# Where the low parts of split weights are made: VectorE alone, or GpSimd in two stages

## The chip, the cores and the metric

The kernel runs on one core of a Trainium2 chip. The core has a matrix engine (PE in the profile), a vector engine (DVE), a scalar engine (ACT), GpSimd (POOL) and a sync engine (SP) that issues the DMAs. The metric is the device time of one execution in microseconds; below it stands as the median of three runs.

## The reference

Two transformer blocks follow each other, each with two layers, on 256 tokens of width 1024 (the first block also carries a second stream of 256 context tokens). Cut to what matters here:

```python
# first block, layer l
h  = modulate(rms_norm(x,  norm1_g[l]), sh1, sc1)      # and hc from the context stream
q, k, v, up, ca, cb = split(h @ w_in[l])               # the same for hc
attn   = diff_attention(rope(q), [kc, rope(k)], [vc, v])
pool_o = pool_mixer(up, ...)
conv_o = conformer_conv(ca, cb, ...)                   # 31 taps, depthwise
x = x + g1 * concat(attn, pool_o, conv_o) @ w_out[l]
x = x + g2 * swiglu(modulate(rms_norm(x, norm2_g[l])), w_ffn_in[l], w_ffn_out[l])
# second block, layer l
c_q, c_kv, k_r, q_d, k_d, v_d = split(rmsnorm(x) @ w_in_2[l])
o_a = mla_mixer(c_q, c_kv, k_r, ...)                   # 8 heads, dense attention
o_b = dilated_attention(q_d, k_d, v_d, rel_bias)       # 8 heads
x = x + concat(o_a, o_b) @ w_out_2[l]
x = x + conv_ffn(rmsnorm(x), w_up_2[l], ...)
```

All of it is in float32.

## The kernel before

A product with a weight is made in three passes on the matrix engine. Weights come in **pieces** of at most 128 x 1024 elements: SP loads a piece into a tile `raw` (four buffers), ACT rounds it into the high part, `hl[:, 0]` (L202), and VectorE subtracts that from `raw` to make the low part, `hl[:, 1]` (L204). `hl` has four buffers as well. The activations have a high and a low part too, and PE adds high x high, high x low and low x high into one PSUM bank (L156). A piece therefore costs ACT one cast, VectorE one subtraction with two inputs in SBUF, and PE its products; PE's first product of a piece needs the high part alone, its second the low part.

`dense` is the loop for a projection: for each piece, for each tile of 128 tokens, for each k-slice of the piece, the three products. In the first layer's q, k and v there are four token tiles and a piece holds two k-slices of 512 columns, so a piece feeds 24 products.

Program order is written with generators. `weave(main, side, rate)` advances the main generator and, for each of its steps, `rate` steps of a side generator. The framework then places the instructions in the engines' queues by their order in the program and by a simulated time at which each becomes ready: an instruction that is ready early can be put ahead of ones that stand before it in the code. Each engine works its queue in order.

Three places matter here.

*The first layer's q, k, v stage* (`layer1` with `l == 0`). Main makes q, k and v out of twelve pieces (two of them already split by `start`); the side runs ten steps of `conv_mix`, the depthwise convolution on VectorE: per channel half 31 taps, one `tensor_scalar` and thirty `scalar_tensor_tensor` (L1236), each 128 x 512 with two inputs in SBUF. Ten steps cover 43 of the 62 taps; the others stand in the side generator of the next weave. After the stage two pieces for the pooling branch are split (`pool_pieces`), then `diff_attention` starts: for each head, score products on PE, a maximum on VectorE (L1297, from PSUM), exponentials on ACT (L1299), a combination on VectorE (L1304), and two heads later transposes and value products on PE.

*The second block's attentions* (`layer2`, both layers). Before them stand the projections to q, k and v of the first attention; their last VectorE steps scale the keys (L1631, L1633) ahead of PE's transposes. Then main runs 8 + 8 heads and the side runs the projection of the second attention's keys (4 pieces), of its values (4 pieces) and the first four pieces of the output projection.

*GpSimd* makes only small reciprocal roots (L162, L163, L421, L422) and memsets in the kernel before.

Of the kernel before, what the change touches and what calls it, by code (L numbers as in the profile page):

```python
# [9 lines left out]
F32 = mybir.dt.float32  # L10
# [87 lines left out]
class _Kernel:  # L98
    def __init__(self, ctx, tc, io, out):
        self.tc, self.nc, self.io, self.out = tc, tc.nc, io, out  # L100
        self.n = 0
        self.last = self.mark = None
        self.later, self.due = [], []
        pool = lambda name, bufs, **kw: ctx.enter_context(tc.tile_pool(name=name, bufs=bufs, **kw))
        self.big = pool("big", 12)
        self.wraw = pool("wraw", 4)
        self.whl = pool("whl", 4)
        self.s4 = pool("s4", 3)
        self.s2 = pool("s2", 6)
        self.small = pool("small", 16)  # L110
        self.cst = pool("cst", 1)
        self.lay = pool("lay", 1)
        self.gatep = pool("gatep", 2)
        self.setp = pool("setp", 1)
        self.junkp = pool("junkp", 1)
        self.conv = pool("convp", 1)
        self.acc = pool("acc", 4, space=bass.MemoryType.PSUM)
        self.aux = pool("aux", 3, space=bass.MemoryType.PSUM)
        self.ob = pool("ob", 1, space=bass.MemoryType.PSUM)
        self.dram = pool("dram", 1, space=DRAM)  # L120
# [73 lines left out]
    def piece(self, view, a, b, mark=None):  # L194

        return self.split(self.load(view, a, b), a, b, mark)

    def split(self, raw, a, b, mark=None):
        nc = self.nc
        n = a * b  # L200
        hl = self.whl.tile([P, 2, 1024], F32R, tag="hl", name=self.nm("hl_"))
        nc.scalar.copy(hl[:, 0, :n], raw[:, :n])  # L202
        with self.behind(mark):
            nc.vector.tensor_sub(hl[:, 1, :n], raw[:, :n], hl[:, 0, :n].bitcast(F32))  # L204
        hi = hl[:, 0, :n].rearrange("p (a b) -> p a b", a=a)
        lo = hl[:, 1, :n].rearrange("p (a b) -> p a b", a=a)
        return hi, lo
# [744 lines left out]
    def layer1(self, l, S, xin, hT, first=()):  # L952

        nc, io = self.nc, self.io
# [16 lines left out]
        def band_load():  # L971
            band = self.A8([P, 2, 4, SEQ])
            for kt in range(2):
                self.dma(band[:, kt], io["k_band"][kt].rearrange("p (g t) -> p g t", g=4))
            return band
# [10 lines left out]
        def values(ready):  # L986
            v.append(self.A8([P, 4, 512]))
            yield from self.dense(
                stat, KD, w_in, 1024, 1536, kv_toks, lambda t, j, b: nc.scalar.copy(v[0][:, t, :], b), ready=ready)

        def main():
            kp, pp, vp = [], [], []
            ahead_v = lambda: vp.append(piece(0, 2, 1024, 1536))
            yield from self.qk_chunk(S, 0, stat, w_in, q_toks, qT, rq, "q_norm_g", first,
                                     lambda: kp.append(piece(0, 2, 512, 1024)))
            yield from self.qk_chunk(S, 1, stat, w_in, kv_toks, kT, rq, "k_norm_g", kp,
                                     (lambda: pp.extend(pool_pieces())) if last else ahead_v)
            if last:
                yield from self.pool_mix(S, stat, 0, band, mB, pp, ahead_v)
            yield from values(vp)  # L1000

        if last:
            band = band_load()
            self.weave(main(), conv, TAPS[l])
        else:

            self.weave(main(), (next(conv) for _ in range(10)), 0.84)
        self.flush()
        v = v[0]
# [4 lines left out]
        def add(gts):  # L1014
            last = [None]

            def evac(t, n, b):
                cs = slice(n * 512, (n + 1) * 512)
                tmp = self.S2([P, 512])
                with self.behind(last[0]):  # L1020
                    nc.vector.tensor_mul(tmp, b, gts[t // 2][:, cs])
                r = res[t // 2][:, t % 2, cs]
                last[0] = nc.vector.tensor_add(r, r, tmp)  # L1023
                return last[0]
            return evac

        hT2 = None
        if not last:
            gates = [self.gate(l, 2, s) for s in streams]

            band, pp = band_load(), pool_pieces()

            def side():
                for s in streams:
                    for _ in self.pool_mix(S, stat, s, band, mB, pp):
                        next(conv, None)
                        yield
                mA.extend(self.parts(TQ))
                for _ in conv:
                    yield  # L1040
                yield from self.ada_rows(l, 2)
                self.rows_to_gates(gates)
                for p, d in ((3, 2), (4, 3)):
                    yield from self.ada_rows(l, p)
                    self.rows_to_cols(S.mod[:, d], S.part(p))

            rf = lambda t: res[t // 2][:, t % 2, :]
            out = self.out_proj(mstat, io["w_out"][l], TQ, add(gates), lambda t: done(t))

            def side_all():  # L1050
                yield from side()
                while not self.fronts:
                    yield
                for _ in range(2):
                    next(out)
                    yield

            self.weave(self.diff_attention(S, qT, kT, v, rq, q_toks, mA, LAG), side_all(), 2.0)
            for s, name in enumerate(("x", "ctx")):
                res[s] = self.reload(name)  # L1060
            G2, S2 = self.modulation(S, l, 1, "n2")
            hT2 = self.norm_out(512)
            done = self.norm_step(rf, G2, S2, hT2)
            for _ in out:
                pass
            g2, nxt = [None, None], []

            def side2():
                yield
                yield  # L1070
                for s in streams:
                    g2[s] = self.gate(l, 5, s)
                nxt.append(self.setup1(l + 1))
                yield from self.ada_sums(l, 5, streams)
                self.sums_to_gates(g2)
                nx = nxt[0]
                nx.rest()
                yield from self.setup2()
                self.gate_next = self.gate(l + 1, 2, 2)
                for p, d, st in ((0, 0, [0, 1]), (1, 1, [0, 1]), (3, 2, [0]), (4, 3, [0])):  # L1080
                    yield from self.ada_sums(l + 1, p, st)
                    self.sums_to_cols(nx.mod[:, d], nx.part(p))
                yield from self.ada_sums(l + 1, 2, [0])
                self.sums_to_gates([self.gate_next])

            end = {}

            def done_ffn(t):
                if t == 0:
                    end["hT"] = self.norm_out(512)  # L1090
                    end["step"] = self.norm_step(rf, *self.modulation(nxt[0], l + 1, 0, "n1"), end["hT"])
                end["step"](t)

            self.weave(
                self.ffn_wide(hT2, io["w_ffn_in"][l], io["w_ffn_out"][l], self.glu(512), add(g2), done_ffn),
                side2(), 0.85)
            return nxt[0], res[0], end["hT"]
# [398 lines left out]
    def layer2(self, l, S, xres, bias, begin):  # L1496
        nc, io = self.nc, self.io
# [147 lines left out]
        def drain(g):  # L1645
            for _ in g:
                pass
# [75 lines left out]
        def main():  # L1723
            yield from attention(
                lambda h, t: qT[0:MQK, h, t * P:(t + 1) * P], lambda h: kT[0:MQK, h, :], mrq, None, 0)
            yield from attention(
                lambda h, t: dqT[sl(h), h // 2, t * P:(t + 1) * P], lambda h: dkT[sl(h), h // 2, :], drq,
                lambda h, t: bias[t][:, h, :], 1)
# [10 lines left out]
        def side():  # L1739
            yield from dil_chunk(1, base + 512, dkT)  # L1740
            self.flush()
            yield from self.dense(
                stat, KD, w_in, base + 1024, base + 1536, toks,
                lambda t, j, b: nc.scalar.activation(vv[:, 1, t, :], b, AF.Identity, scale=rs[t]))
            while len(turned) < 4:
                yield
            for _ in range(4):
                next(out)
                yield
                yield  # L1750

        self.weave(main(), side(), 1.2)
        drain(out)
        nxt, end = [], {}

# [54 lines left out]
```

## Time and profile before

| what | value |
|---|---|
| median of three runs | 1667.15 us (1663.48 to 1668.55) |
| the profiled execution's own time | 1667.61 us |
| its span, first to last instruction | 1665.8 us |
| PE busy | 1618.0 us (97%) |
| VectorE busy | 1180.4 us (71%) |
| ACT busy | 793.9 us (48%) |
| GpSimd busy | 43.8 us (3%) |
| TensorE's granted clock, mean | 0.983 of full speed |
| subtractions L204 on VectorE | 382, busy 457.8 us |

Busy is the share of the span in which an engine had an instruction under way; a busy PE may still be waiting inside a group of products. The time before and after the span (1667.61 less 1665.8) is 1.8 us.

### The profile page before, as it was taken

The numbers are of one execution on the slowest core, as the hardware profiler recorded it, in microseconds if no ns is written. First come the engines' busy times: TensorE is split into PE (matmuls) and PEld (weight loads), VectorE is DVE, ScalarE is ACT, GpSimd is POOL, SyncE is SP. The second block draws the span as 40 slices with busy tenths as digits, with TensorE's granted clock in tenths as the row PEclk, the third lists the DMA queues.
The fourth block names the chain that finished last, engine by engine and source line by source line (L and its number), as shares of the span: only waits on it lengthen the run. The fifth ranks groups of instructions, "written<-read, shape, count | busy, mean of one in ns | idle before, by whom it ended". The sixth has DMA issues, their size and how long they took to land.

```text
span 1665.8 us, 24269 instructions
## 1 busy us (share of the span) xinstructions
PE 1618.0 (97%) x9241; PEld 1354.8 (81%) x9241; DVE 1180.4 (71%) x2130; ACT 793.9 (48%) x1347; POOL 43.8 (3%) x99
## 2 busy tenths in 40 slices
PE   7999999999999999999799899999999999999999
PEld 5787568878888888886698899767999987689998
DVE  4796656856575555986566457877887888778786
ACT  4334436323222224655543346765555577665554
POOL 1000000000000000000000001000000010000000
PEclk8999979999999999999899999999999999999999
DMA  9421651745375553432369655432656554246553
GB/s 329 129 89 59 245 177 55 225 148 168 108 228 174 175 153 113 140 114 82 99 224 243 194 188 159 151 102 88 204 181 190 177 150 150 87 128 189 189 181 122
DMA packets 183011, 262.71 MB, mean 158 GB/s; under 512 B 11277, under 2 KB 122864, under 8 KB 182896
## 3 DMA queue, kind: packets, MB, share of 16 engines
q1 hardware_dynamic: 182616, 260.85, 50.1%
q8 instruction: 72, 1.18, 0.3%
q10 hardware_dynamic: 280, 0.33, 0.2%
q14 instruction: 43, 0.35, 0.1%
HBM read 259.84 MB, written 1.31 MB: 157 GB/s over the span
## 4 chain that ended last, share of the span: by engine, by line
PE 69%; DVE 12%; issue 8%; DMA 6%; ACT 3%; POOL 1%; SPq 0%; POOLq 0%; ACTq 0%; DVEq 0%
PE aux L156 34%; PE acc L156 27%; PE ob L156 6%; DVE hl L204 3%; DMA raw<-in_w_mod_dram 3%; PE aux L248 2%; DVE a L1236 2%; DVE s L1236 1%; ACT hl L202 1%; DMA a<-dbias 1%; DMA raw<-in_w_ffn_out_dram 1%; DVE s L355 1%; DMA raw<-in_w_in_dram 1%; ACT s L461 1%; DVE sm L843 1%
## 5 line engine op out<-in xcount | busy, mean ns | idle before, releaser
L156 PE MATMUL acc<-hl,a 128*128 128x512 f32 (+3 forms) x3072 | 720.4, 387 | 8.1 <-ACT hl L202 2.9
L156 PEld LDWEIGHTS acc<-hl,a 128*128 128x128 f32 x3072 | 553.5, 190 | 127.2 <-issue 15.5
L202 ACT CAST hl<-raw 128x1024 fp32r<-128x1024 f32 (+2 forms) x382 | 393.6, 1036 | 473.5 <-PE aux L156 141.4
L156 PE MATMUL aux<-a,hl 128*128 128x256 f32 (+1 forms) x4032 | 578.5, 304 | 8.1 <-ACT a L462 2.9
L156 PEld LDWEIGHTS aux<-a,hl 128*128 128x128 f32 x4032 | 539.4, 192 | 41.5 <-ACT a L462 3.7
L204 DVE TENSOR_TENSOR hl<-raw,hl 128x1024 fp32r<-128x1024 f32 (+2 forms) x382 | 457.8, 1203 | 162.0 <-ACT hl L202 160.3
L355 DVE SCALAR_TENSOR_TENSOR s<-raw,csf,s 128x1024 f32<-128x1024 f32 x70 | 88.7, 1281 | 46.8 <-DMA raw<-in_w_mod_dram 46.7
L248 PEld LDWEIGHTS aux<-km,s 128*128 128x128 f32 (+1 forms) x384 | 45.2, 143 | 35.9 <-issue 20.1
L248 PE MATMUL aux<-km,s 128*128 128x128 f32 (+1 forms) x384 | 60.0, 284 | 12.3 <-DVE s L443 8.0
L156 PE MATMUL ob<-a,hl 128*128 128x512 f32 (+1 forms) x288 | 64.3, 372 | 0.0
L156 PEld LDWEIGHTS ob<-a,hl 128*128 128x128 f32 x288 | 51.2, 188 | 9.4
L524 ACT ACTIVATE s<-aux 128x512 f32<-128x512 f32 x33 | 19.7, 598 | 66.0 <-PE aux L156 66.0
L552 ACT ACTIVATE s<-s,c2a,c2b 128x256 f32<-128x256 f32 x88 | 48.0, 593 | 5.9 <-DVE s L549 5.9
L527 ACT CAST a<-s 128x512 fp32r<-128x512 f32 x33 | 20.4, 618 | 54.9 <-DVE s L526 54.8
L549 DVE TENSOR_TENSOR s<-aux,km 128x512 f32<-128x512 f32 x44 | 30.4, 691 | 20.5 <-PE aux L156 20.5
L1236 DVE SCALAR_TENSOR_TENSOR a<-up,c,a 128x512 f32<-128x512 f32 x60 | 43.5, 748 | 0.5
L525 DVE SCALAR_TENSOR_TENSOR s<-s,aux 128x512 f32<-128x512 f32 x33 | 22.6, 685 | 29.4 <-ACT s L524 29.4
L248 PE MATMUL aux<-km,a 128*128 128x128 f32 (+1 forms) x196 | 31.1, 289 | 10.5 <-ACT a L770 7.9
L409 ACT ACTIVATE jk<-a 128x512 bf16<-128x512 f32 x44 | 28.1, 640 | 25.2 <-DVE a L1023 19.7
L553 DVE SCALAR_TENSOR_TENSOR s<-s,c2a,s 128x255 f32<-128x255 f32 x88 | 38.7, 479 | 1.4 <-ACT s L552 1.4
L248 PEld LDWEIGHTS aux<-km,a 128*128 128x128 f32 (+1 forms) x196 | 23.7, 146 | 18.6 <-ACT a L770 8.1
L555 DVE SCALAR_TENSOR_TENSOR s<-s,c2b,s 128x255 f32<-128x255 f32 x88 | 38.7, 480 | 0.1
(257 smaller groups left out, 1364.3 us busy)
## 6 DMA issues: line engine op xcount, KB each, us to landing
raw<-in_w_ffn_in_dram SPq DMA_DIRECT2D x88, 512.0 KB
raw<-in_w_up_dram SPq DMA_DIRECT2D x88, 512.0 KB
raw<-in_w_in_dram SPq DMA_DIRECT2D x60, 512.0 KB
raw<-in_w_mod_dram SPq DMA_DIRECT2D x56, 512.0 KB
raw<-in_w_ffn_out_dram SPq DMA_DIRECT2D x44, 512.0 KB
raw<-in_w_down_dram SPq DMA_DIRECT2D x44, 512.0 KB
wm<-in_w_mod_dram SPq DMA_DIRECT2D x16, 1024.0 KB
raw<-in_w_out_dram SPq DMA_DIRECT2D x32, 512.0 KB
```

The source lines that it names most:

```text
L156: self.nc.tensor.matmul(o, lhsT, rhs, start=start, stop=stop)
L202: nc.scalar.copy(hl[:, 0, :n], raw[:, :n])
L204: nc.vector.tensor_sub(hl[:, 1, :n], raw[:, :n], hl[:, 0, :n].bitcast(F32))
L248: self.nc.tensor.transpose(b[:rows, j * P:(j + 1) * P], s, self.ident)
L355: self.nc.vector.scalar_tensor_tensor(accs[s], raw, c, accs[s], op0=ALU.mult, op1=ALU.add)
L409: self.nc.scalar.activation(junk, x[:, h * 512:(h + 1) * 512], AF.Square, scale=D ** -0.5, accum_out=ss[:, h:h + 1])
L525: nc.vector.scalar_tensor_tensor(th, th, 1.0, g, op0=ALU.add, op1=ALU.mult)
L549: nc.vector.tensor_mul(y, x.rearrange("p (j t) -> p j t", j=2), R2)
L552: nc.scalar.activation(o[:, j, :], y[:, j, :], AF.Identity, scale=wc(1, ff), bias=bc(ff))
L553: nc.vector.scalar_tensor_tensor(o[:, j, 1:SEQ], y[:, j, 0:SEQ - 1], wc(0, ff), o[:, j, 1:SEQ], op0=ALU.mult, op1=ALU.add)
L555: nc.vector.scalar_tensor_tensor(o[:, j, 0:SEQ - 1], y[:, j, 1:SEQ], wc(2, ff), o[:, j, 0:SEQ - 1], op0=ALU.mult, op1=ALU.add)
L1236: nc.vector.scalar_tensor_tensor(o, up[:, ct, :, k:k + SEQ], w, o, op0=ALU.mult, op1=ALU.add)
```

## The change

A member `self.low` names the engine that makes the low parts. It is VectorE at first, GpSimd from the start of the first layer's q, k, v stage until the pooling pieces are split, and GpSimd again in the weave of the second block's two attentions, in each of its two layers. Counted from the code, that moves 10 + 2 subtractions in the first layer and 12 in each layer of the second block, 36 of 382, all of 128 x 1024.

```diff
+        self.low = self.nc.vector
...
         nc.scalar.copy(hl[:, 0, :n], raw[:, :n])
         with self.behind(mark):
-            nc.vector.tensor_sub(hl[:, 1, :n], raw[:, :n], hl[:, 0, :n].bitcast(F32))
+            self.low.tensor_sub(hl[:, 1, :n], raw[:, :n], hl[:, 0, :n].bitcast(F32))
...
         else:
+            self.low = nc.gpsimd
             self.weave(main(), (next(conv) for _ in range(10)), 0.84)
...
             band, pp = band_load(), pool_pieces()
+            self.low = nc.vector
...
+        self.low = nc.gpsimd
         self.weave(main(), side(), 1.2)
+        self.low = nc.vector
         drain(out)
```

## Rows read from the trace of the kernel before

**Rows 1.** The page's part 1: busy us, share of span, instructions.
```profile
PE 1618.0 (97%) x9241; PEld 1354.8 (81%) x9241; DVE 1180.4 (71%) x2130; ACT 793.9 (48%) x1347; POOL 43.8 (3%) x99
```

**Rows 2.** The page's part 4: the chain that ended last, by engine.
```profile
PE 69%; DVE 12%; issue 8%; DMA 6%; ACT 3%; POOL 1%; SPq 0%; POOLq 0%; ACTq 0%; DVEq 0%
```

**Rows 3.** Windows: length, busy us of PE, PEld, DVE, ACT, POOL; clock; DMA share; GB/s.
```profile
61.00:131.00 70.00, 69.88 (x323) 57.20 (x321) 69.20 (x137) 26.83 (x41) 0.20 (x1) 1.00 0.33 106
131.00:140.00 9.00, 7.19 (x27) 4.49 (x27) 8.93 (x18) 4.88 (x9) 0.00 (x0) 0.81 0.37 117
...
1062.00:1142.00 80.00, 79.57 (x386) 55.82 (x384) 57.33 (x155) 50.72 (x115) 0.00 (x0) 1.00 0.31 99
```

**Rows 4.** Groups of VectorE by line and shape: busy us, mean ns, idle before.
```profile
L204 DVE TENSOR_TENSOR hl<-raw,hl 128x1024 fp32r<-128x1024 f32 x360 | 438.6, 1223 | 157.9 <-ACT hl L202 156.2
```

**Rows 5.** Timeline of VectorE, first layer: start us, length us, line, operation.
```profile
66.26 1.22 DVE L204 TENSOR_TENSOR hl<-raw,hl 128x1024 fp32r<-128x1024 f32 x1
67.40 0.74 DVE L1236 SCALAR_TENSOR_TENSOR a<-up,c,a 128x512 f32<-128x512 f32 x1
...
115.05 1.22 DVE L204 TENSOR_TENSOR hl<-raw,hl 128x1024 fp32r<-128x1024 f32 x1
...
120.12 12.56 DVE L1236 SCALAR_TENSOR_TENSOR a<-up,c,a 128x512 f32<-128x512 f32 x16
132.60 1.28 DVE L1297 TENSOR_REDUCE sm<-acc 128x1 f32<-128x512 f32 x2
...
135.31 1.22 DVE L204 TENSOR_TENSOR hl<-raw,hl 128x1024 fp32r<-128x1024 f32 x1
```

**Rows 6.** Timeline of PE where the first attention starts; idle before in brackets.
```profile
131.09 1.13 PE L156 MATMUL acc<-a,a 64*128 64x512 f32 x4
132.78 0.38 PE L156 MATMUL acc<-hl,a 128*128 128x256 f32 x1 [0.56 <-ACT hl L202]
...
134.96 1.12 PE L156 MATMUL acc<-a,a 64*128 64x512 f32 x2 [0.75 <-ACT s L1299]
136.59 7.17 PE L156 MATMUL acc<-hl,a 128*128 128x256 f32 x47 [0.50 <-DVE hl L204]
```

**Rows 7.** Timeline of ACT: casts that make high parts.
```profile
108.10 1.05 ACT L202 CAST hl<-raw 128x1024 fp32r<-128x1024 f32 x1
...
131.68 1.05 ACT L202 CAST hl<-raw 128x1024 fp32r<-128x1024 f32 x1
...
1055.11 1.05 ACT L202 CAST hl<-raw 128x1024 fp32r<-128x1024 f32 x1 [1.51 <-PE acc L156]
```

**Rows 8.** Windows behind PE's gap at 132 to 136 us, columns as in Rows 3.
```profile
136.00:138.00 2.00, 1.50 (x7) 1.42 (x7) 2.00 (x3) 0.62 (x2) 0.00 (x0) 0.53 0.00 0
138.00:140.00 2.00, 2.00 (x13) 2.00 (x12) 2.00 (x7) 0.78 (x2) 0.00 (x0) 0.62 0.00 0
```

**Rows 9.** Groups of GpSimd by line and shape: busy us, mean ns, idle before.
```profile
L162 POOL TENSOR_SCALAR sm<-sm 128x4 f32<-128x4 f32 x5 | 1.0, 194 | 85.5 <-DVE sm L1327 48.3 <-ACT s L1313 21.2 <-DVE sm L1255 16.0
...
L665 POOL MEMSET poolw<- 128x256 f32 x2 | 0.6, 312 | 16.8 <-PE aux L156 16.8
...
L275 POOL MEMSET mean_w<- 128x128 f32 x1 | 0.2, 206 | 0.3 <-POOLq L1796 0.3
```

**Rows 10.** Timeline of GpSimd, second block.
```profile
1036.14 0.76 POOL L162 TENSOR_SCALAR sm<-sm 128x1 f32<-128x1 f32 x1 [1.20 <-ACT jk L1524]
...
1150.46 1.57 POOL L421 TENSOR_SCALAR sm<-sm 128x1 f32<-128x1 f32 x1
```

**Rows 11.** Timeline of VectorE over the same moments.
```profile
1035.62 1.23 DVE L204 TENSOR_TENSOR hl<-raw,hl 128x1024 fp32r<-128x1024 f32 x1
...
1150.73 1.22 DVE L204 TENSOR_TENSOR hl<-raw,hl 128x1024 fp32r<-128x1024 f32 x1
```

**Rows 12.** Timeline of VectorE: keys scaled ahead of the second block's first attention.
```profile
1056.53 0.42 DVE L1633 TENSOR_TENSOR a<-a,sm 128x256 f32<-128x256 f32 x1
```

**Rows 13.** Timeline of PE: the transposes of these keys.
```profile
1057.09 1.05 PE L248 MATMUL aux<-km,a 128*96 128x128 f32 x8
```

## The prediction

> **What bounds the kernel now.** I read the page first. PE is busy for 97% of the span, VectorE for 71%, GpSimd for 3% [rows 1], and the chain that ended last runs through PE for 69% of the span and through VectorE for 12% [rows 2]. So moving VectorE's work pays only where VectorE stands in front of PE. The windows of the three stages say where. From 61 to 131 us, the first layer's q, k and v, PE has 69.88 of 70 us and VectorE 69.20: both are full, and PE doesn't wait [rows 3]. From 131 to 140 us PE has only 7.19 of 9 us, VectorE 8.93, and the granted clock is 0.81 of full. In the second block's attentions (1062 to 1142 us; the other layer repeats it 324 us later) PE has 79.57 of 80 us and VectorE 57.33 [rows 3]: there is almost nothing to win.
>
> The timelines around 131 us show the only visible loss. PE makes its first score products at 131.09, but VectorE is still working off sixteen convolution taps and takes up their maximum at 132.60, with no idle time ahead of it [rows 5, 6]. PE then waits for ACT's exponentials until 134.96, and until 136.59 for the low part of the first pooling piece [rows 6]: its cast began at 131.68 [rows 7], its subtraction at 135.31, because other work stood ahead of it in VectorE's queue [rows 5]. [...]
>
> **What is removed.** 36 of the 382 subtractions leave VectorE. One takes 1.22 us [rows 4], and the next instruction starts 1.14 us after it (66.26 to 67.40) [rows 5]. That is 11.4 us for the ten ahead of the first attention, 2.3 us for the two pooling pieces, 13.7 us in each layer of the second block; 41.0 us in all. As PE is full in those stages, most of it is worth nothing by itself.
>
> **What is added.** GpSimd makes 36 subtractions of 128 x 1024 with two inputs in SBUF. No row shows one. Nearest are its memsets: 206 ns for 128 elements per partition, 312 ns for 256 [rows 9], or 0.83 ns an element for writing alone. For 1024 elements one pass is 0.85 us and three (two reads and a write) are 2.55 us; with the 0.19 us of an instruction that moves nearly nothing [rows 9], the bounds are 1.0 and 2.7 us. I estimate 2.3 us, nearer the upper end, since no row shows the passes of one instruction overlapping. [...]
>
> That length is harmless to PE by itself. A piece feeds 24 products here, and PE gets pieces about three ahead: the last cast of v's pieces is at 108.10 and its subtraction at 115.05, 7 us late, and PE didn't notice [rows 5, 7]. GpSimd has nothing else to do in these stages [rows 3]. ACT's casts and the SP queue issue the same instructions as before; a `raw` buffer is free when its subtraction ends, which is no later than now where VectorE was 7 us behind.
>
> **What it does to VectorE.** The rows show that the two engines don't run freely beside each other. A GpSimd `tensor_scalar` on a few elements takes 0.19 us [rows 9]; at 1036.14 one takes 0.76 us and ends 0.05 us after a VectorE subtraction that runs from 1035.62 to 1036.85, and at 1150.46 one takes 1.57 us and ends 0.08 us after one that runs until 1151.95 [rows 10, 11]. So GpSimd waits for a VectorE instruction with two SBUF inputs. Whether VectorE waits for a long GpSimd instruction in the same way the trace can't show, as GpSimd has none. Bounds for one moved subtraction: VectorE loses nothing, or the whole 2.7 us of the upper bound. I take 1.8 us: an exclusion that holds one way probably holds the other way, and a fifth of the 2.3 us is covered by VectorE's other instructions (the reductions, such as L1297, have one input), beside which no row shows GpSimd waiting.
>
> [...]
>
> **The sum, first layer.** VectorE's arrival at the first maximum (132.60) moves by: minus 11.4 us for ten subtractions; plus 18.0 us for ten blocks of 1.8 us; plus 2.7 us, because the remaining four of 62 taps (two stand behind 132.60 ahead of the pooling subtraction, two later) will be put ahead of it, at 0.67 us each, once VectorE looks free earlier; minus 1.9 us, because sixteen taps that now run alone at 0.785 us (12.56 us [rows 5]) run among other work at about 0.67. That is plus 7.4 us: 140.0. The engines' order comes from a simulated readiness, so taps are drawn forward whether or not VectorE really has the time. From the maximum to the third pair of score products takes 2.36 us (132.60 to 134.96) and the pair itself 1.1; the pooling products can resume at 143.5, against 136.59 [rows 5, 6]. Plus 7 us. With nothing lost the maximum would start at 131.4, when its product is ready, and the gap would shrink by 1.5 us, with up to 1.7 us of clock given back (2 us at 0.53 and 2 us at 0.62); with the full 2.7 us per block the plus is 16.
>
> **The sum, second block.** In the attentions VectorE sheds 13.7 of some 57 us and takes on up to 12 blocks; the heads' transposes come two heads after their scores, which covers a few microseconds, and PE stays full. The tight place is ahead of it. L1633 ends at 1056.95, and PE's transposes of these keys begin at 1057.09 [rows 12, 13]. The cast of the first moved piece ends at 1056.16 [rows 7], so its 2.3 us on GpSimd fall on L1633 or on the root and scaling for the second token tile, which feed the next transposes. VectorE's own subtraction of 1.14 us leaves that place. I estimate plus 1 us per layer, with minus 1 and plus 4 as bounds; two layers: plus 2.
>
> Total: 7 + 2 = plus 9 us on the profiled execution's 1667.61, so 1676.6. That execution is 0.46 us above the median of the runs; against the median the forecast is 1676.
>
> **The rivals.** *Free ride* (the other side): VectorE's accesses slip between GpSimd's. Then nothing is blocked, VectorE has idle time ahead of 131 us, the pooling piece's low part comes at 132.73 + 2.3 = 135.0 instead of 136.54, and the clock doesn't fall so far: minus 3 in the first layer, minus 1 per layer of the second block, so about 1662 (1659 to 1666). For it: VectorE's subtractions beside GpSimd take 1.22 and 1.23 us [rows 11], the mean of all of them being 1.223 [rows 4]; against it: those GpSimd instructions touch one element. It decides from a block below about 1.06 us, where ten blocks, four taps and the saved spacing cancel the 11.4 us freed.
>
> *Yielding*: VectorE goes first every time, as in both rows of GpSimd's waits, and GpSimd's subtractions stretch to 4 or 5 us. The lead of three pieces hides that, VectorE still gains its time, but the first pooling piece comes no earlier than now: 1667 (1664 to 1670).
>
> *Starving*: GpSimd gets through so seldom between taps that its low parts come later than the lead covers, and PE waits for them: 36 pieces with 1 us each would give 1703. Against it: GpSimd got in right behind the VectorE instruction it waited for.
>
> **How the numbers follow.** What a measurement of this kernel can tell from no change is about 0.3%, or 5 us. Blocked both ways, as forecast: 0.47 (0.42 beyond 5 us, 0.05 within). Free ride: 0.35, of which 0.20 is beyond 5 us and 0.15 within. Yielding: 0.15, all within. Starving: 0.03, slower. So faster 0.20, same 0.35, slower 0.45. The likeliest case alone ranges from 1669 (blocks of 1.2 us) to 1686 (blocks of 2.7 us and a few microseconds in the second block). To leave out no more than 2 in 10 the range takes in most of the free ride: 1661 to 1686.
>
> **What the profile after would show.** Twelve GpSimd tensor_tensor in the first layer, twelve in each second-block stage, 2.3 us or more each; VectorE's taps between 61 and 131 us with single ones stretched from 0.75 us to 2 us or more; the first maximum after 138 us, and PE idle ahead of it; in 1055 to 1062 us later transposes. If taps keep 0.75 us and the maximum starts at about 131.4, the forecast is wrong and the free ride right. If GpSimd's subtractions are 4 us and VectorE's durations unchanged, it is the yielding one. If GpSimd's instruction is near 1 us, blocks are too short to matter. A changed order of other queues could move a few microseconds either way that I have not priced.

## The result and the profile after

The changed kernel takes 1727.53 us (median of four runs; 1724.21 to 1727.89), the kernel before, run beside it, 1666.58 us: ratio 1.0361, 95% interval 1.0348 to 1.0373. That is slower, as forecast, by 61 us where 9 were forecast, and 41 us beyond the upper end of the range. In the listings from here on most lines stand two to four numbers higher than before (the product L156 is L158, the cast L202 is L204, the subtraction L204 is L206, the tap L1236 is L1240, the maximum L1297 is L1301).

The page's part 1, which answers to [rows 1], and its chain by engine, to [rows 2]:

```profile
PE 1631.6 (95%) x9241; PEld 1362.4 (79%) x9241; DVE 1198.0 (69%) x2094; ACT 794.7 (46%) x1347; POOL 151.6 (9%) x135
...
PE 69%; DVE 13%; issue 9%; ACT 4%; DMA 3%; POOL 1%; SPq 0%; POOLq 0%; ACTq 0%; DVEq 0%
```

VectorE issues 36 instructions fewer and is busy 18 us longer: its own instructions have become longer. GpSimd's new instruction, in the view of one tile (ns: least, median, most), and who waited for it:

```profile
L206 POOL TENSOR_TENSOR hl<-raw,hl x36: 2339/2390/15470, 63.2 to 1484.2; 128x1024 fp32r<-128x1024 f32 x36
...
  PEld acc L158: 1.8, 1
  PE acc L158: 1.0, 1
```

2.34 us at the least, 2.39 in the median; 15.47 us once and 9.01 us once. PE waited for its results 2.8 us in all, so late low parts are not where 61 us went. The two GpSimd instructions of [rows 10], which stand at the two ends of the second block's first attention, tell where:

```profile
1055.09 0.75 POOL L164 TENSOR_SCALAR sm<-sm 128x1 f32<-128x1 f32 x1 [1.21 <-ACT jk L1528]
...
1189.40 1.56 POOL L423 TENSOR_SCALAR sm<-sm 128x1 f32<-128x1 f32 x1
```

From the one to the other it is 134.31 us now and was 114.32 (1150.46 less 1036.14): plus 20.0. The first of the pair came at 1036.14 and comes at 1055.09, so some 19 us were lost earlier; the second layer loses another 20 between 1400 and 1533 us. The three stages that the change touches lose about 20 us each, and the rest of the program nothing. Windows of these stages (columns as in [rows 3]), and then the window of the kernel before in which PE has as many products as in the last one:

```profile
61.00:89.00 28.00, 28.00 (x125) 22.81 (x123) 27.50 (x46) 11.50 (x17) 22.57 (x5) 1.00 0.19 57
89.00:105.00 16.00, 3.88 (x14) 3.18 (x14) 16.00 (x28) 1.63 (x2) 8.81 (x4) 0.60 0.74 259
105.00:132.00 27.00, 27.00 (x123) 22.12 (x121) 26.06 (x46) 9.15 (x14) 14.35 (x3) 0.99 0.07 23
132.00:142.00 10.00, 6.28 (x28) 5.14 (x27) 8.56 (x17) 3.31 (x5) 0.19 (x2) 0.83 0.01 2
1068.00:1149.00 81.00, 67.69 (x298) 50.20 (x299) 53.12 (x141) 42.32 (x86) 28.73 (x12) 0.89 0.31 98
```

```profile
1049.00:1110.00 61.00, 60.62 (x298) 46.27 (x299) 46.84 (x153) 42.07 (x86) 0.00 (x0) 1.00 0.42 130
```

PE, full until 131 us before, is idle for 12.1 of the 16 us from 89 us on, for 3.7 us of the ten from 132 us on, and for 13.3 of 81 us in the second block. There the mean granted clock is 0.89 besides. By estimate that costs 0.11 of 67.69 us, or 7.4 us; with 12.9 us more of idle time (13.3 by 0.4 in the 61 us of before) it makes 20.3, about the 20.0 that were measured.

The first layer, PE's timeline (brackets: idle time before, and what ended it), then VectorE's, and last q's first sum in the kernel before:

```profile
101.33 1.12 PE L250 MATMUL aux<-km,a 128*128 128x128 f32 x4 [12.12 <-DVE a L857]
...
135.98 0.64 PE L250 MATMUL aux<-km,a 128*128 128x128 f32 x4 [3.73 <-DVE a L864]
...
150.93 1.13 PE L158 MATMUL acc<-a,a 64*128 64x512 f32 x4
154.87 0.38 PE L158 MATMUL acc<-hl,a 128*128 128x256 f32 x1 [2.81 <-ACT hl L204]
```

```profile
72.65 14.66 DVE L1240 SCALAR_TENSOR_TENSOR a<-up,c,a 128x512 f32<-128x512 f32 x22
87.24 0.67 DVE L845 TENSOR_REDUCE sm<-s 128x8 f32<-128x512 f32 x1
87.84 2.28 DVE L1240 SCALAR_TENSOR_TENSOR a<-up,c,a 128x512 f32<-128x512 f32 x1
90.04 0.67 DVE L845 TENSOR_REDUCE sm<-s 128x8 f32<-128x512 f32 x1
90.64 4.98 DVE L1240 SCALAR_TENSOR_TENSOR a<-up,c,a 128x512 f32<-128x512 f32 x2
...
96.13 1.96 DVE L854 TENSOR_TENSOR s<-a,ropeB 128x256 f32<-128x256 f32 x1
...
137.56 3.11 DVE L1240 SCALAR_TENSOR_TENSOR a<-up,c,a 128x512 f32<-128x512 f32 x4
152.09 0.69 DVE L1301 TENSOR_REDUCE sm<-acc 128x1 f32<-128x512 f32 x1 [11.42 <-PE acc L158]
```

```profile
80.88 0.68 DVE L843 TENSOR_REDUCE sm<-s 128x8 f32<-128x512 f32 x1
```

Read them together. Twenty-two taps run back to back ahead of q's first sum (L845), which begins 6.4 us later than before: 23 taps stand ahead of it in all, where 15 did, and the making of the rotary tables (L682, L687) is held for 6.6 us. Then each sum lets a GpSimd subtraction in, and the VectorE instruction behind the sum takes about 2 us or more: taps of 2.28 us and 4.98 us for two, by 0.75 us each before, and a rotary product (L854) of 1.96 by 0.42. PE's transposes of q stand behind the last of that chain (L857) in PE's queue, and PE waits 12.12 us. The attention's first products come at 150.93 us, 19.8 us later than in [rows 6], and the first maximum finds VectorE idle for 11.42 us.

The second block's first attention, around one head, in the timeline of all engines:

```profile
1103.37 1.12 PE L250 MATMUL aux<-km,s 128*128 128x128 f32 x4 [3.29 <-ACT s L1686]
...
1103.68 1.06 ACT L204 CAST hl<-raw 128x1024 fp32r<-128x1024 f32 x1
1104.16 0.68 DVE L1676 TENSOR_REDUCE sm<-aux 128x2 f32<-128x512 f32 x1
...
1104.82 2.36 POOL L206 TENSOR_TENSOR hl<-raw,hl 128x1024 fp32r<-128x1024 f32 x1 [2.81 <-ACT hl L204]
1104.88 2.31 DVE L1677 SCALAR_TENSOR_TENSOR sm<-sm,mrq 128x2 f32<-128x2 f32 x1
...
1107.31 0.56 ACT L1686 ACTIVATE s<-aux,sm,mrq 128x256 f32<-128x256 f32 x1 [2.57 <-DVE sm L1677]
```

L1677 multiplies two columns of two elements. It took at most 0.17 us before; here it starts 0.06 us behind a GpSimd subtraction and ends with it. The next instruction of its head, ACT's exponential, waits, and on the first line PE's transposes have just waited 3.29 us for the exponential of an earlier head, which had been delayed in the same way. ACT's cast, which releases the subtraction, ends just as the head's maximum (L1676) is being taken. From 1066 to 1148 us ACT waited 14.7 us for L1677; before, where the same instruction is L1673, 5.7 (microseconds in all, times, the longest):

```profile
ACT s L1686 <- DVE sm L1677: 14.7, 6, 2.9
```

```profile
ACT s L1682 <- DVE sm L1673: 5.7, 5, 2.0
```

### The profile page after: what moved, and what is told of

It reads as the page before. It is cut to its first block, busy times and chain, and to the rows that moved or that the text cites. A ratio compares the mean times of both kernels' runs of the same rounds, so it can differ in the third digit from the quotient of the medians.

```text
span 1725.3 us, 24266 instructions
## 1 busy us (share of the span) xinstructions
PE 1631.6 (95%) x9241; PEld 1362.4 (79%) x9241; DVE 1198.0 (69%) x2094; ACT 794.7 (46%) x1347; POOL 151.6 (9%) x135
## 4 chain that ended last, share of the span: by engine, by line
PE 69%; DVE 13%; issue 9%; ACT 4%; DMA 3%; POOL 1%; SPq 0%; POOLq 0%; ACTq 0%; DVEq 0%
PE aux L158 35%; PE acc L158 26%; PE ob L158 6%; PE aux L250 3%; DVE hl L206 2%; DVE a L1240 1%; DVE s L1240 1%; ACT hl L204 1%; DMA raw<-in_w_mod_dram 1%; DVE sm L176 1%; DMA raw<-in_w_in_dram 1%; ACT s L463 1%; DVE sm L1677 1%; DVE sm L175 1%; DVE sm L177 1%
## 5 line engine op out<-in xcount | busy, mean ns | idle before, releaser
L158 PE MATMUL acc<-hl,a 128*128 128x512 f32 (+3 forms) x3072 | 730.1, 390 | 11.0 <-ACT hl L204 5.2
L158 PEld LDWEIGHTS acc<-hl,a 128*128 128x128 f32 x3072 | 557.3, 191 | 133.4 <-issue 17.9
L204 ACT CAST hl<-raw 128x1024 fp32r<-128x1024 f32 (+2 forms) x382 | 393.3, 1036 | 481.0 <-PE aux L158 146.2
L158 PE MATMUL aux<-a,hl 128*128 128x256 f32 (+1 forms) x4032 | 578.8, 304 | 7.5 <-ACT a L464 2.9
L158 PEld LDWEIGHTS aux<-a,hl 128*128 128x128 f32 x4032 | 539.7, 192 | 41.0 <-ACT a L464 3.7
L206 DVE TENSOR_TENSOR hl<-raw,hl 128x1024 fp32r<-128x1024 f32 (+2 forms) x346 | 413.7, 1201 | 163.3 <-ACT hl L204 161.3
L206 POOL TENSOR_TENSOR hl<-raw,hl 128x1024 fp32r<-128x1024 f32 x36 | 107.7, 3000 | 146.4 <-ACT hl L204 146.4
L423 POOL TENSOR_SCALAR sm<-sm 128x1 f32<-128x1 f32 x22 | 10.5, 478 | 780.6 <-ACT jk L411 780.3
L250 PE MATMUL aux<-km,a 128*128 128x128 f32 (+1 forms) x196 | 34.9, 312 | 35.0 <-DVE a L857 12.1
L158 PE MATMUL ob<-a,hl 128*128 128x512 f32 (+1 forms) x288 | 64.3, 372 | 0.0
L158 PEld LDWEIGHTS ob<-a,hl 128*128 128x128 f32 x288 | 51.2, 188 | 9.4
L1240 DVE SCALAR_TENSOR_TENSOR a<-up,c,a 128x512 f32<-128x512 f32 x60 | 48.7, 861 | 0.1
```

Of the source, the lines that this page charges most:

```text
L158: self.nc.tensor.matmul(o, lhsT, rhs, start=start, stop=stop)
L206: self.low.tensor_sub(hl[:, 1, :n], raw[:, :n], hl[:, 0, :n].bitcast(F32))
L250: self.nc.tensor.transpose(b[:rows, j * P:(j + 1) * P], s, self.ident)
L1240: nc.vector.scalar_tensor_tensor(o, up[:, ct, :, k:k + SEQ], w, o, op0=ALU.mult, op1=ALU.add)
```

## The experiments

Each time is a median; the kernel before ran beside them (1665.5 to 1666.6 us). The third column is the start of GpSimd's first root in the first attention (157.38 us before), the fourth the stretch of [rows 10] (114.32 us before).

| kernel | us (ratio, 95% interval) | first root | second block |
|---|---|---|---|
| changed kernel | 1727.53 (1.0348 to 1.0373) | 178.84 | 134.31 |
| e1_first | 1689.01 (1.0123 to 1.0153) | 179.78 | 114.30 |
| e2_second | 1706.17 (1.0227 to 1.0261) | 158.81 | 134.72 |
| e3_write | 1677.13 (1.0047 to 1.0089) | 164.83 | 115.63 |
| e7_ghost_read | 1727.68 (1.0356 to 1.0387) | 181.77 | 134.20 |
| e7_ghost_write | 1666.72 (0.9999 to 1.0018) | 157.24 | 114.43 |
| e4_quarters | 1704.66 (1.0214 to 1.0248) | 180.13 | 123.28 |
| e5_onein | 1694.64 (1.0159 to 1.0196) | 158.20 | 127.66 |
| e6_onein_dve | 1667.59 (1.0001 to 1.0019) | 157.83 | 114.50 |
| e9_hold_dve | 1682.22 (1.0084 to 1.0115) | 174.73 | not touched |
| e10_hold_pool | 1690.08 (1.0135 to 1.0163) | 182.39 | not touched |
| e8_pool_only | 1666.90 (0.9995 to 1.0013) | 158.33 | not touched |
| e11_taps_behind | 1666.00 (0.9995 to 1.0012) | another order | not touched |

**The halves.** The theory at this point, drawn from the rows above (L1677 with 2.31 us by 0.17, a tap with 2.28 by 0.75): a GpSimd instruction that reads SBUF shuts out VectorE's instructions with two SBUF inputs, and what is shut out stands in the chains for which PE waits. The rivals: low parts that come too late, and the changed order of the queues. First, whether the stages are independent.

```diff
-        self.low = nc.gpsimd
+        self.low = nc.vector
         self.weave(main(), side(), 1.2)
```

> GpSimd makes the 12 low parts of the first layer alone; the second block's stay on VectorE. If the three stages lose independently, as the landmarks of the changed kernel say (+20 us at the first attention's norms, then +20 in each layer of the second block): before plus 20, about 1687 us, and the second block's two stages as long as before (61 us for 1049 to 1110). If the loss is one of the whole kernel (a lower clock throughout, or transfers that fall behind), the second block's stages are longer here too and the time is not 1687.

The other half makes the same replacement ahead of the first layer's weave and leaves this one.

> GpSimd makes the 24 low parts of the second block's attentions alone. Independent stages: before plus 40, about 1707 us, and the two effects of this run and its sibling add up to the whole 61 us. If not: a sum that misses 61 us by more than 6.

1689 and 1706 us: plus 23.4 and plus 40.6, together 64 us where both at once cost 61, and neither lengthens the other's stage by more than 1.4 us. The stages are independent within some 3 us.

**Writes in place of reads.** GpSimd is busy in the same places for about as long, and PE's second product of a piece waits for it, but it hardly reads. The kernel leaves out the low parts of the 36 pieces.

```diff
-            self.low.tensor_sub(hl[:, 1, :n], raw[:, :n], hl[:, 0, :n].bitcast(F32))
+            if self.low is nc.vector:
+                nc.vector.tensor_sub(hl[:, 1, :n], raw[:, :n], hl[:, 0, :n].bitcast(F32))
+            else:
+                for w in (n, n, n // 4):
+                    nc.gpsimd.memset(raw[:, :w], 0.0)
+                nc.gpsimd.tensor_mul(hl[:, 1, :8], raw[:, :8], hl[:, 0, :8].bitcast(F32))
...
-        lo = hl[:, 1, :n].rearrange("p (a b) -> p a b", a=a)
+        lo = (hl[:, 1, :n] if self.low is nc.vector else hl[:, 1, 0:1].to_broadcast([P, n])).rearrange("p (a b) -> p a b", a=a)
```

> In the 36 places GpSimd only writes: three memsets over the raw tile (1024, 1024 and 256 columns, some 2.1 to 2.4 us together), then a multiplication of 8 columns that makes a low part of zeros, which PE reads through a broadcast. It leaves out the low parts of these 36 pieces. The order of all queues is that of the changed kernel but for a few rows, and the low part comes as late as there. Blocking theory (GpSimd's reads of two inputs shut out VectorE's instructions with two SBUF inputs): VectorE's small two-input instructions return to 0.15 us and the taps to 0.75 us, and the time is that of before or a little under, 1658 to 1672 us. Rival, the low parts come too late for PE, or the changed order of the queues costs it: 1715 to 1730 us, as in the changed kernel. If GpSimd's writes shut VectorE out as well: 1700 or more, with VectorE instructions stretched by one memset, 0.9 us.

1677 us: 50 of the 61 us are gone, and the forecast for the theory (1672 at most) is missed by 5. The second block is back to within 1.3 us. The first layer keeps 7.5 us. This kernel has the changed order too: the same 22 taps stand back to back ahead of q's first sum. PE's waits at the transposes of q and k, 12.12 and 3.73 us in the changed kernel, are small here:

```profile
90.39 0.66 PE L250 MATMUL aux<-km,a 128*128 128x128 f32 x4 [0.74 <-DVE a L857]
...
92.56 0.66 PE L250 MATMUL aux<-km,a 128*128 128x128 f32 x4 [0.61 <-DVE a L857]
...
120.91 0.63 PE L250 MATMUL aux<-km,a 128*128 128x128 f32 x4 [0.97 <-DVE a L864]
```

That is 2.3 us. Besides, ACT casts the first pooling piece behind the attention's first exponential, and PE waits 2.81 us for it, as in the changed kernel (154.87), by 0.56 in [rows 6]. So the order has a price of its own, small beside the holds. The multiplications of 8 columns, which read two inputs, also waited; this view of one tile shows one of 5.8 us where 0.2 is usual:

```profile
L206 POOL TENSOR_TENSOR hl<-raw,hl x36: 202/214/5755, 67.9 to 1438.1; 128x8 fp32r<-128x8 f32 x36
```

**Reads and writes that nobody waits for.** This pair takes both rivals out: VectorE keeps all its subtractions, PE waits for nothing new, and PE, VectorE, ACT and SP have the order of the kernel before.

```diff
-            self.low.tensor_sub(hl[:, 1, :n], raw[:, :n], hl[:, 0, :n].bitcast(F32))
+            nc.vector.tensor_sub(hl[:, 1, :n], raw[:, :n], hl[:, 0, :n].bitcast(F32))
+            self.low is nc.gpsimd and nc.gpsimd.tensor_sub(raw[:, :n], raw[:, :n], hl[:, 0, :n].bitcast(F32))
```

> VectorE makes all low parts, as before, in the order of before on every queue; in the 36 places GpSimd subtracts once more, into the raw tile, which nobody reads after. PE waits for nothing that is new. Blocking theory: VectorE waits up to 2.35 us for each of the 36, without having shed its own subtractions: 1710 to 1750 us. Rival (late low parts, or the order): nothing is late and nothing is reordered, so 1667 us within 5; a freed raw buffer comes some 3 us later, which the transfers' lead covers.

> The pair of the run in which GpSimd subtracts once more into the raw tile: the same 36 places, the same waits, the same order on PE, VectorE, ACT and SP, but GpSimd only writes (memsets of 1024, 1024 and 256 columns over the raw tile, 2.33 us together). Blocking by reads: VectorE is not held and the time is that of before, 1667 us within 5. If GpSimd's writes hold VectorE as its reads do, or if it is the later release of the raw tile that cost the pair's 62 us: 1715 to 1730 us.

1727.68 and 1666.72 us. Useless subtractions on GpSimd cost 62 us; useless writes of the same length in the same places cost nothing that can be measured. Windows of the run that reads (the first layer, then the second block), and of the one that writes:

```profile
61.00:131.00 70.00, 61.03 (x264) 49.56 (x262) 69.16 (x106) 22.40 (x33) 26.59 (x10) 0.93 0.28 91
1070.00:1151.00 81.00, 65.63 (x297) 49.12 (x296) 64.99 (x152) 43.21 (x88) 28.52 (x12) 0.94 0.31 98
```

```profile
61.00:131.00 70.00, 69.88 (x325) 57.23 (x323) 69.29 (x137) 26.76 (x40) 22.05 (x31) 1.00 0.33 106
1049.00:1130.00 81.00, 80.52 (x391) 58.45 (x389) 63.06 (x184) 53.27 (x114) 26.57 (x36) 1.00 0.39 119
```

GpSimd is about as busy in the one as in the other (26.59 and 22.05 us in the first layer, 28.52 and 26.57 in the second block); in the second block PE has 65.63 us of 81 beside reads and 80.52 beside writes. This pair shows that reads are enough for the whole loss, with nothing late and nothing reordered, and that writes in their place are not. That a memset is shorter than a subtraction (0.95 us by 2.39) is not the reason: subtractions cut to 0.74 us each, in the next run, still cost 39 us.

The run that reads also answers for the first layer. No tap is drawn forward in it, and PE waits 17.6 us at the transposes of q and k, by 15.9 in the changed kernel:

```profile
97.62 1.12 PE L250 MATMUL aux<-km,a 128*128 128x128 f32 x4 [8.08 <-DVE a L857]
...
139.60 1.94 PE L250 MATMUL aux<-km,a 128*128 128x128 f32 x8 [9.49 <-DVE a L864]
```

**Shorter holds.** The changed kernel with each GpSimd subtraction cut in four; the other engines' order is the same.

```diff
-            self.low.tensor_sub(hl[:, 1, :n], raw[:, :n], hl[:, 0, :n].bitcast(F32))
+            step = n if self.low is nc.vector else n // 4
+            for c in [slice(i, i + step) for i in range(0, n, step)]:
+                self.low.tensor_sub(hl[:, 1, c], raw[:, c], hl[:, 0, c].bitcast(F32))
```

> The changed kernel with each GpSimd subtraction in four of 256 columns; the order of the other queues is the same. One takes about 0.7 us by the whole one's 2.35 us. If it is the length of a single hold that costs (a tiny instruction in a head's chain waits 2.35 us), the second block's plus falls from 20 us per layer to 5 to 12, while the first layer, where VectorE is full and loses the same sum of time, keeps 15 to 25: 1692 to 1712 us in all. If only the sum of GpSimd's time counts: 1727 us or more, since four instructions together take longer than one.

1704.66 us. Both parts came out: the second block's plus falls from 20.0 to 9.0 us per layer, the first layer's stays (180.13, plus 22.7). One instruction takes 0.74 us in the median, 2.96 us for four by 2.39 for a whole one, and the time falls all the same. The view of the tile, and the window of the second block:

```profile
L206 POOL TENSOR_TENSOR hl<-raw,hl x144: 718/740/8038, 61.9 to 1464.1; 128x256 fp32r<-128x256 f32 x144
```

```profile
1068.00:1149.00 81.00, 72.05 (x348) 52.62 (x348) 54.28 (x162) 48.57 (x102) 36.40 (x48) 1.00 0.36 112
```

PE's idle time in this window, 8.95 us of 81, is the whole plus of 9.0, at a clock of 1.00. So of the 11.0 us that come back in each layer some 4 are PE's idle time (13.31 by 8.95), and the rest is about what the clock had taken. In the second block it is the latency of one hold in a head's chain that costs, not the sum of GpSimd's time.

**One held instruction taken out.** GpSimd in the second block alone, with L1677 rewritten.

```diff
-                    nc.vector.scalar_tensor_tensor(nm, mx, -1.0, rr, op0=ALU.mult, op1=ALU.mult)
+                    for t in toks:
+                        nc.vector.tensor_scalar(nm[:, t:t + 1], mx[:, t:t + 1], rr[:, t:t + 1], -1.0, op0=ALU.mult, op1=ALU.mult)
```

> GpSimd in the second block alone (1706 us by itself), and the product L1677 of two tiny SBUF inputs (128 x 2) in the first attention's heads becomes two instructions with one tensor input and a per-partition scalar. If a hold falls on two-input instructions only, these take 0.17 us each and never wait for GpSimd; ACT's wait for them, 14.7 us in the first layer's stage of the changed kernel, goes, and the time falls by 6 to 20 us, to 1686 to 1700. The other two-input instructions of the chain (L1692, the roots of L175 to L177) are still held, so not all 40 us come back. If any VectorE instruction is held: 1706 us or a little more.

> The control of the run before it in this list: the same replacement of L1677, all low parts on VectorE. Both theories: 16 more tiny instructions on a VectorE that is not the bound there, so 1667 us within 5.

1694.64 us, 11.5 less than without the rewriting; on the kernel before it changes 0.1%. GpSimd's and VectorE's timelines show the two one-element instructions running inside a subtraction, 0.69 us after its start, and in the view of waits ACT's wait for L1677 fell to 7.6 us, from 13.9 without the rewriting (14.7 in the changed kernel, 5.7 in the kernel before):

```profile
1081.05 2.38 POOL L206 TENSOR_TENSOR hl<-raw,hl 128x1024 fp32r<-128x1024 f32 x1 [3.23 <-ACT hl L204]
```

```profile
1081.74 0.33 DVE L1677 TENSOR_SCALAR sm<-sm,mrq 128x1 f32<-128x1 f32 x2
```

```profile
ACT s L1686 <- DVE sm L1677: 7.6, 6, 3.0
```

The plus per layer is still 13.3 us: the roots (L175 to L177) and the scaling of the exponentials (L1692) are held as before (L177 for 2.37 us at 1099.96, L1692 for 1.30 at 1119.58, by 0.16 and 0.69).

**The first layer's place.** All taps are made to stand behind the rotary embedding of q's second token tile, once with the low parts on VectorE, once with the first layer's on GpSimd.

```diff
-            nc.vector.tensor_add(sv, sv, tmp)
+            self.hold = nc.vector.tensor_add(sv, sv, tmp) if which == 0 else nc.vector.tensor_add(sv, sv, tmp) and self.hold
...
-            self.weave(main(), (next(conv) for _ in range(10)), 0.84)
+            self.weave(main(), (i >= 5 and next(conv) for i in range(15)), 0.84)
...
-                    nc.vector.scalar_tensor_tensor(o, up[:, ct, :, k:k + SEQ], w, o, op0=ALU.mult, op1=ALU.add)
+                    with self.behind(self.hold):
+                        nc.vector.scalar_tensor_tensor(o, up[:, ct, :, k:k + SEQ], w, o, op0=ALU.mult, op1=ALU.add)
```

> Half of a pair. All low parts on VectorE, but every convolution tap stands behind the rotary embedding of q's second token tile, so none is ahead of q's sums; 21 taps then stand ahead of the attention's first maximum (16 in the kernel before). The first maximum comes 2 to 5 us later than its 132.60 us: 1667 to 1674 us.

> The other half: the same hold on the taps, and the first layer's 12 low parts on GpSimd. If the first layer lost because holds and 22 taps drawn forward fell on q's sums and rotary embedding, for which PE's transposes wait (12.12 us at 101.33 in the changed kernel), that wait falls under 3 us and this run is at most 8 us above its other half. Rival, the sum of VectorE's time in the stage decides, wherever the holds fall: ten holds of 1.7 us against 11.4 us shed, which with the clock's loss would be some 20 us above the other half, as the first layer alone was (1689 us against 1666).

The first is 16 us slower than the kernel before, not 7 at most: its first maximum comes at 133.69, only 1.1 us later, but 12 taps of 8.04 us then stand ahead of the second head's maxima, which I had not counted. The second is 7.9 us above it, where the first layer on GpSimd cost 23 without the hold. PE's waits at the transposes of q and k, where the first of the pair has none:

```profile
90.23 0.66 PE L250 MATMUL aux<-km,a 128*128 128x128 f32 x4 [0.36 <-DVE a L857]
94.25 1.11 PE L250 MATMUL aux<-km,a 128*128 128x128 f32 x4 [3.36 <-DVE a L857]
...
125.95 0.63 PE L250 MATMUL aux<-km,a 128*128 128x128 f32 x4 [2.32 <-DVE a L864]
```

6.0 us by 15.9 in the changed kernel; the wait for q, 3.7 us, is a little over the 3 I gave it. VectorE has time to spare in this kernel (it is busy for 41.95 us of the 70 from 61 to 131 us), and holds in q's and k's chains still cost PE 6 us. The pair takes away two things at once, the taps ahead of q's sums and VectorE's lack of slack, so by itself it doesn't tell which of them the other 10 us need. The earlier runs do in part: the order, almost without the holds, made PE wait 2.3 us at these transposes (e3_write), and the holds alone, on a VectorE that is full in the order of before, 17.6 us (e7_ghost_read). That the taps drawn forward matter mainly because they keep VectorE full is likely, but no run shows it by itself.

**Two versions that might have gained.** GpSimd for the pooling pieces alone, and a kernel without GpSimd in which the last seven taps stand behind the first maximum.

> GpSimd makes the low parts of the two pooling pieces alone, in front of whose subtractions VectorE had other work in the kernel before (PE waited 0.50 us for the first). Blocking: the first GpSimd subtraction starts beside the maxima and holds L1302 or a tap for up to 2.35 us, so the first heads' exponentials come 1 to 2 us later: plus 0 to 4 us, 1666 to 1671. Rival, here it is a gain, since the low part comes 1.5 us earlier than VectorE brings it: 1662 to 1665.

> A version without GpSimd: the kernel before, with 55 of the 62 taps woven ahead of the first attention and the last 7 behind its first maximum, so that 13 taps stand between the keys' scaling and that maximum instead of 16. The first maximum comes about 2 us earlier and PE's waits of 0.56, 0.75 and 0.50 us shrink; with the clock's share at most 3 us: 1663 to 1667 us.

Neither differs from the kernel before by as much as can be told. In the first, the low part follows its cast at once, but L1302 is held (1.37 us by 0.15) and the second piece comes later than before: PE's waits of 0.56, 0.75 and 0.50 us [rows 6] become 0.56, 0.98 and 1.34. In the second VectorE is no longer late (1.94 us idle ahead of the maximum), but PE waits 2.35 us for ACT's cast instead. No version that I ran beats the kernel before.

## Why the prediction was wrong

The direction and the mechanism were right; the places where the holds fall were wrong, and with them the size.

- **GpSimd's time:** estimated 2.3 us (bounds 1.0 to 2.7); measured 2.34 at the least, 2.39 in the median. Right.
- **Blocking both ways:** assumed by symmetry, shown by the pair of useless reads and writes: 62 us for the reads, and for the writes about 1 us (1666.72 us by 1665.52; interval 0.9999 to 1.0018), which can't be told from nothing. The free ride and the yielding rival fall with it. The starving rival falls by another number: GpSimd did starve (15.47 us behind 22 back-to-back taps, 9.01 behind 16), but PE waited only 2.8 us for low parts.
- **The sum of VectorE's time in the first layer:** right. The held instructions between 61 and 131 us are longer than before by 16.9 us (three in the making of the rotary tables 2.20, 2.20 and 2.23; taps 1.53, 3.56, 0.52 and 1.54; rotary products 1.54 and 1.61), 1.7 us per subtraction by the 1.8 of the forecast. VectorE was ready for the first maximum at 140.67 (137.56 plus 3.11); I had said 140.0. That the forecast comes so close here is partly luck: its sum had no GpSimd subtraction that waits out a run of taps, and took more kinds of VectorE instruction for cover than are free (see the last section).
- **Where that reaches PE: the step that failed in the first layer.** I let VectorE's lateness meet PE only at the first maximum, for plus 7 us, because PE had not noticed a subtraction 7 us late. The holds, and the taps drawn ahead of q's sums, fell on q's and k's rotary chains, and PE's transposes stand in PE's queue behind these: 12.12 and 3.73 us of idle time, and by estimate 2.6 us more through a granted clock of 0.60 from 89 to 105 us (0.40 of 3.88) and 0.83 from 132 to 142 (0.17 of 6.28). The first products came 19.8 us late, with VectorE waiting for PE; the later cast added 2.3 us behind them (2.81 by 0.56). I had seen that taps are drawn forward, but counted them against the total, not against the sums that they were put ahead of; the holds are the larger part (17.6 us of waits without that order, 2.3 us with it and almost without the holds).
- **The second block: the step that failed outright.** I wrote that the transposes come two heads after their scores, that this covers a few microseconds, and that PE stays full: plus 1 us per layer (minus 1 to plus 4) for the place ahead of the attention. That place alone took 4.33 us of PE's idle time (at 1079.24 us, for roots held through two subtractions of 5.00 us together). Most of the rest of 12.9 fell on the heads (1.83 us on a scaling of the second attention's keys, L1576, woven in beside them): each has a chain of two-input instructions, a few elements each, and ACT's queue puts the cast that releases a GpSimd subtraction right behind one head's exponentials, so that it begins when the next head's L1677 is due. I priced holds in proportion to VectorE's busy time, and an instruction of 0.15 us has none to speak of. The quarters show that it is latency: 9.0 instead of 20.0 us with more GpSimd time in all. The forecast of plus 2 us for both layers met plus 40.
- **The clock** is no term of the forecast's sum; only the case with nothing lost gives some of it back, up to 1.7 us in the first layer [rows 8]. In the second block it took about 7 us per layer, by the estimate above.

What stays open: why the clock was lower in one stretch with gaps and not in another (1.00 with PE at 72.05 of 81 us in the quarters, 0.89 with 67.69). I measured it and did not experiment on it.

## What to carry to other kernels

Before moving elementwise work with SBUF inputs from VectorE to GpSimd, list VectorE's instructions in that stage that the profile puts on a chain ahead of PE, down to those of 0.15 us and with the one-input kinds of the last section, and price each with one whole GpSimd instruction of waiting (here 2.31 us on one of 0.15). VectorE's idle share doesn't help: the stage with 28% of it lost as much as the one with 1%. If GpSimd has to do it, short instructions lose less in chains (9.0 by 20.0 us here), and work that only writes cost nothing here that could be measured.

## What the runs showed of the hardware

A one-input VectorE instruction can be held too. I had taken these for cover. Reductions and reciprocals ran freely inside GpSimd's subtractions, as L845 and L1676 did at 0.68 us and L1691 at 0.17, but some `tensor_scalar` and copies of 8 or 32 fp32 elements per partition did not. GpSimd's timeline and VectorE's, in the run of useless reads, twice:

```profile
107.25 2.93 POOL L206 TENSOR_TENSOR raw<-raw,hl 128x1024 f32<-128x1024 f32 x1 [1.26 <-DVE hl L206]
...
1100.74 2.40 POOL L206 TENSOR_TENSOR raw<-raw,hl 128x1024 f32<-128x1024 f32 x1 [3.04 <-DVE sm L177]
```

```profile
107.84 2.38 DVE L879 COPY rq<-sm 128x32 f32<-128x32 f32 x1
...
1100.79 2.38 DVE L179 TENSOR_SCALAR sm<-sm 128x8 f32<-128x8 f32 x1
```

Both end with the subtraction; alone they take 0.15 to 0.18 us. The `tensor_scalar` of one element per partition that replaced L1677 was not held (0.33 us for two of them, inside a subtraction of 2.38). So of the fp32 copies and `tensor_scalar` in these rows, those of 8 and 32 elements were held and that of one element was not; why, no run shows.

These one-input instructions are held by writes too. In the run of useless writes two of three memsets, 0.95 us each, hold them to their end:

```profile
1069.62 2.33 POOL L206 MEMSET raw<- 128x1024 f32 x3 [1.12 <-DVE hl L206]
```

```profile
1069.67 0.92 DVE L179 TENSOR_SCALAR sm<-sm 128x8 f32<-128x8 f32 x1
...
1070.63 0.98 DVE L1573 COPY drq<-sm 128x8 f32<-128x8 f32 x1
```

Two-input instructions of the same size ran in 0.17 us beside a memset of that run (L176 at 1056.80, L177 at 1057.00), and the taps between 61 and 160 us took 759 ns in the mean, by 748 in the kernel before and 944 in the run of useless reads. So writes are not without any hold; in these places the holds were short (0.92 and 0.98 us here) and cost no time that could be measured.

The hold works the other way at length: a GpSimd subtraction that begins beside 22 VectorE taps without a gap (at 74.10) gets in when the one-input sum (L845) behind them begins, at 87.24; it ends 2.33 us after that, 15.47 us after its own start, by 2.39 undisturbed.
